# A two-layer decoder trunk on one core: one weight split of layer B's output projection is queued behind the exponentials of the fourteenth head

## The chip, the cores and the metric

The kernel runs on one core of a Trainium2 chip. Its engines have queues of their own and wait for each other through semaphores: TensorE (PE: matmuls and transposes; PEld: its weight loads), VectorE (DVE), ScalarE (ACT), GpSimd (POOL), and SyncE (SP), which issues most of the DMA loads. The metric is the device time of one execution in microseconds; it was 991.41 us before the change, as the median of three runs (990.88 to 992.49).

## The reference, cut to what matters

Two layers over 512 tokens of width 1024, all in float32. Layer A has latent attention and an MLP. Layer B, where the change lies, has sliding-window attention with 16 query heads on 4 key/value heads, each with a learned sink, then the output projection `w_o`, a layer norm and another MLP.

```python
def _swa(x, w_q, sinks, w_o, k_band, v_band, rel_bias):
    q = (x @ w_q).reshape(B, nb, BLOCK, SWA_KV_HEADS, G, SWA_HEAD_DIM)
    s = jnp.einsum('bnqkgd,bnjkd->bnkgqj', q, k_band).astype(jnp.float32) * SWA_HEAD_DIM ** -0.5
    ...
    s = jnp.where(mask[None, :, None, None], s + bias, -jnp.inf)
    m = jnp.maximum(s.max(-1), sink)
    p = jnp.exp(s - m[..., None])
    denom = p.sum(-1) + jnp.exp(sink - m)
    p = (p / denom[..., None]).astype(x.dtype)
    o = jnp.einsum('bnkgqj,bnjkd->bnqkgd', p, v_band).reshape(B, S, SWA_Q_HEADS * SWA_HEAD_DIM)
    return o @ w_o
...
x = _layernorm(alpha * x + y, ln_mix_g[l], ln_mix_b[l])
x = _layernorm(alpha * x + _mlp(x, mlp_w_up[l], mlp_w_down[l]), ln_mlp_g[l], ln_mlp_b[l])
```

## The kernel before

**Products in two parts.** Every float32 operand is split into a high part that the matrix unit takes and a low part, what is left: `split` (line 75) copies on ACT (line 77) and subtracts on DVE or POOL (line 81). A product is then three matmuls, high by high, high by low and low by high (`three`); all matmuls are written by `group` (line 105), so that one line of the profile holds nearly all of PE.

**The weights' stream.** All weights come as chunks of 128 by 1024 in one list, `stream`, in the order of their use. `queue` (line 128) appends a chunk: its `make` loads it into a `raw` tile (two buffers; the load is issued on SP, line 142) and splits it into `wh` and `wl` (four buffers each). Whoever needs a chunk calls `weights`, which takes the next one and first prepares chunks until four are on the way. `queue` has an argument `after`: the name of an instruction kept in `state`, and `behind` then makes every instruction of the split that runs on that instruction's engine stand behind it in that engine's order (an edge of order, no wait for its end). For layer B the list has two chunks of `w_k`, two of `w_v`, eight of `w_sq` (the queries) and eight of `w_so` (the output projection), then the MLP's. The low parts of `w_so` are made on POOL for the chunks 0, 1, 2, 6 and 7 (`POOL_SO`), else on DVE. Chunks 6 and 7 are loaded ahead into a tile of their own (line 151).

**The heads.** `run_steps` walks the 16 heads (counted from 0). In step u it writes `scores` of head u + 2, then what is due of a list `fill` (query projections, parts of the output projection, loads), then `turn` of head u, and after every second head `mix` of a pair of heads two steps back.

- `scores`: eight small matmuls into two PSUM banks; DVE puts the window's two halves together (line 1426), adds the bias and takes the maximum (1430), and makes the negative maximum `nb` (1434). `weigh`: ACT takes four exponentials, one for each block of 128 tokens (1440), then the sink's (1445); DVE adds and inverts the sums (1446, 1447), and POOL scales (1449).
- `turn`: PE transposes (1465), ACT and DVE split into `pt` (77, 81), and POOL makes the product with a triangle, `pm` (1469).
- `mix`: matmuls with the values, first into a bank of the pool of two (`tr`), then into one of the pool of six (`mm`), which scores use too; ACT copies a part, `low` (1497), DVE adds, `o` (1499), and ACT and POOL split `o` into `oh` and `ol`.
- `queries`: a projection for two heads; ACT and DVE make `q` (1398, 1399).
- `proj.part(t, kp)`: six matmuls of the output projection for token block t with chunk kp. In the first part, due in step 11, `weights` is called for chunk 0, and chunk 3, the fourth, is prepared: scores of head 13 have then just been written. Chunk 3 itself is multiplied in `proj.finish`, behind all heads.

**What sets the order.** PE's instructions and SP's loads keep the order in which they are written (`pe`). For ACT, DVE and POOL the order is made as the program is built, by a planner that goes through the program with times of its own and puts an instruction into its engine's queue when its operands are ready by those times; edges like that of `behind` bind it. On the chip each engine follows that order strictly: an instruction that waits holds up what is queued behind it.

Of the kernel before, what the change touches and what calls it, by code (L numbers as in the profile page):

```python
# [33 lines left out]
POOL_O, POOL_SO = (0, 2), (0, 1, 2, 6, 7)  # L34
# [14 lines left out]
def build(tc, nc, io, out):  # L49
    with ExitStack() as top:  # L50
# [11 lines left out]
        def nm(s):  # L62
            n_names[0] += 1
            return f"{s}_{n_names[0]}"
# [10 lines left out]
        def split(dst_h, dst_l, src, engine=None, keep=False):  # L75

            high = nc.scalar.activation(dst_h, src, AF.Copy)  # L77
            if keep:
                pe(high)
            with behind(state.pop("open", None)):  # L80
                low = (engine or nc.vector).tensor_sub(dst_l, src, f32(dst_h))  # L81
            if pinned[0] and engine is None:
                pe(low)
            return high, low

        def pe(ins):
            tc.keep_in_program_order(ins)
# [3 lines left out]
        def behind(pair):  # L91

            both = ExitStack()
            for ins in pair or ():
                both.enter_context(tc.issue_after(ins.ins))
            return both
# [20 lines left out]
        def tiles_of_weights(aside=None):  # L117

            if aside:
                return aside()  # L120
            wh = wp.tile([P, 1024], F32R, tag="wh", bufs=4, name=nm("wh"))
            wl = wp.tile([P, 1024], F32R, tag="wl", bufs=4, name=nm("wl"))
            return wh, wl

        def raw_tile():
            return wp.tile([P, 1024], F32, tag="raw", bufs=2, name=nm("raw"))

        def queue(name, ap, low=nc.vector, after=None):


            index = len(stream)

            def make(pieces=1, between=None):
                cols = ap.shape[-1]
                raw = at_hand.pop(index) if index in at_hand else raw_tile()
                wh, wl = tiles_of_weights()
                for j in range(pieces):
                    c = slice(j * cols // pieces, (j + 1) * cols // pieces)
                    if between:
                        between(j)  # L140
                    if index not in fetched:
                        state["load", name] = nc.sync.dma_start(raw[:, c], ap[:, c])
                        pe(state["load", name])
                    with behind((state[after],) if after else None):
                        state["plain"] = split(wh[:, c], wl[:, c], raw[:, c], low)
                return wh, wl

            def fetch(raw):
                at_hand[index] = raw
                fetched.add(index)  # L150
                pe(nc.sync.dma_start(raw[:, : ap.shape[-1]], ap))

            fetchers[index] = fetch
            stream.append((name, make))
            off_ring.append(False)
# [128 lines left out]
        def mlp_stream(l):  # L284
            holds.append(len(stream) + 2)
            def up(q):

                return lambda r, c, jp: io["up"][
                    l, q * 8 + 4 * c + 2 * jp : q * 8 + 4 * c + 2 * jp + 2, :, r * 512 : (r + 1) * 512
                ].rearrange("c p x -> p c x")  # L290

            def down(q):
                return lambda r, c, jp: io["down"][l, q * 8 + 4 * c + 2 * (1 - r) + jp].rearrange(
                    "p (a b) -> p a b", a=2
                )

            add = {("U", q): queue_seven("up", "U", up(q)) for q in range(NFF)}
            add |= {("D", q): queue_seven("down", "D", down(q)) for q in range(NFF - 1)}
            preloads.append(add["U", 0].preload)
            for i, (which, q, n) in enumerate(steps_of()):  # L300
                if i < 2:
                    add[which, q](n, [lambda j=2 * i + jp: aside_of(j) for jp in range(2)])
                else:
                    add[which, q](n)
            for c in range(8):
                queue("down", io["down"][l, (NFF - 1) * 8 + c])
# [8 lines left out]
            queue("w_sq", io["w_sq"][m], nc.gpsimd if m > 1 else nc.vector)  # L315
        first_so = len(stream)
        for c in range(8):
            queue("w_so", io["w_so"][c], nc.gpsimd if c in POOL_SO else nc.vector)
        mlp_stream(1)

        ready = {}
        state = {"next": 0, "at": 0, "hold": 0}
# [637 lines left out]
        with tc.tile_pool(name="mla", bufs=1) as mp:  # L960
# [212 lines left out]
            for t, rs in ((0, (0, 1)), (1, (0, 1)), (0, (2,)), (1, (2,)), (2, range(3)), (3, range(3))):  # L1173
# [3 lines left out]
                for r in rs:  # L1177
                    wh, wl = ws[r // 2]
                    c = slice((r % 2) * 512, (r % 2 + 1) * 512)
# [136 lines left out]
        with tc.tile_pool(name="swa", bufs=1) as mp:  # L1316
# [87 lines left out]
            def scores(h, _):  # L1404
# [17 lines left out]
                for n2 in range(2):  # L1422
# [4 lines left out]
                    for a in range(2):  # L1427
# [5 lines left out]
                        )  # L1433
                nc.vector.tensor_scalar(nb, mx, sink8[:, h : h + 1], -SWA_SCALE, ALU.max, ALU.mult)
                weigh(h, bs, nb, sm, ri)

            def weigh(h, bs, nb, sm, ri):
                p = mp.tile([P, NT, P], F32, tag="p", bufs=3, name=nm("p"))
                for n in range(NT):
                    nc.scalar.activation(  # L1440
                        p[:, n, :], bs[n // 2][:, n % 2, P:], AF.Exp, bias=nb[:, n : n + 1],
                        scale=SWA_SCALE, accum_out=sm[:, n : n + 1],
                    )
                own = bs[0][:, 0, NT : 2 * NT]
                nc.scalar.activation(own, nb, AF.Exp, bias=sink[:, h : h + 1])
                nc.vector.tensor_add(sm, own, sm)
                nc.vector.reciprocal(ri, sm)
                with tc.high_priority():
                    muls[h] = nc.gpsimd.tensor_mul(p, p, ri.unsqueeze(2).broadcast_to([P, NT, P]))
                ps_of[h] = p  # L1450
# [194 lines left out]
```

## Time and profile before

| | |
|---|---|
| runs, median (lowest to highest) | 991.41 us (990.88 to 992.49) |
| the profiled execution: time / span of the trace | 993.6 us / 991.8 us |
| mean granted PE clock | 0.996 |
| PE busy | 981.9 us (99%) |
| DVE busy | 770.5 us (78%) |
| ACT busy | 544.7 us (55%) |
| POOL busy | 238.9 us (24%) |
| head exponentials (line 1440), first to last start | 539.4 to 616.8 us |

Times in the views are microseconds from the start of the span. In a timeline row stand start, duration, engine, line, operation, then the tiles written and read; brackets give the engine's idle time before it and what ended that. The granted clock is the share of the TensorE clock that the throttle let through.

### The profile page before, as it was taken

How to read it: one execution, taken by the hardware profiler on the slowest of the kernel's cores; microseconds unless marked ns; L12 is line 12 of the kernel's file. 1: busy time of each engine (PE TensorE's matmuls, PEld its weight loads, DVE VectorE, ACT ScalarE, POOL GpSimd, SP SyncE). 2: the span in 40 equal slices, each digit the busy share in tenths (PEclk: the TensorE clock that was granted, in tenths of full speed). 3: DMA queues.
4: the chain of work that ended last, by engine and by line, in shares of the span. 5: the costliest groups of instructions: out<-in, count | busy, mean ns of one | idle time of the engine just before them, and what ended most of it. 6: DMA issues, size and time to landing. Idle time of an engine off the chain costs nothing.

```text
span 991.8 us, 15665 instructions
## 1 busy us (share of the span) xinstructions
PE 981.9 (99%) x6028; PEld 883.7 (89%) x6028; DVE 770.5 (78%) x1279; ACT 544.7 (55%) x842; POOL 238.9 (24%) x207
## 2 busy tenths in 40 slices
PE   9999999999999999999999998999999999999998
PEld 9888888998999999998898987889998998999986
DVE  6589858989768769786686787698885986898756
ACT  5557644467547547646146786436763663664620
POOL 0231101121212212210002996512121122023000
PEclk9999999999999999999999998999999999999999
DMA  7431236399779977964132223328996796898332
GB/s 262 138 95 43 89 124 199 57 221 235 139 192 233 169 166 222 228 108 147 65 107 96 86 83 141 113 58 140 279 182 120 235 213 118 222 261 146 85 128 85
DMA packets 60678, 149.54 MB, mean 151 GB/s; under 512 B 5259, under 2 KB 10300, under 8 KB 60604
## 3 DMA queue, kind: packets, MB, share of 16 engines
q0 software_dynamic: 24320, 58.73, 33.4%
q1 hardware_dynamic: 36140, 89.56, 26.0%
q8 instruction: 47, 0.77, 0.3%
q10 hardware_dynamic: 144, 0.26, 0.1%
q14 instruction: 27, 0.22, 0.1%
HBM read 146.41 MB, written 4.22 MB: 152 GB/s over the span
## 4 chain that ended last, share of the span: by engine, by line
PE 97%; DMA 1%; DVE 1%; POOL 0%; ACT 0%; issue 0%; SPq 0%; DVEq 0%; POOLq 0%
PE mm L105 89%; PE tr L105 5%; PE tr L1243 1%; DMA raw<-in_w_so 1%; PE tr L742 1%; PE tr L1465 1%; PE tr L507 0%; POOL wl L81 0%; PE tr L1007 0%; PE mm L1148 0%; ACT p L1440 0%; DVE pt L81 0%; DVE mm L1430 0%; DVE x L481 0%; ACT wh L77 0%
## 5 line engine op out<-in xcount | busy, mean ns | idle before, releaser
L105 PE MATMUL mm<-wh,fac 128*128 128x512 f32 (+1 forms) x944 | 292.5, 386 | 0.0
L77 ACT ACTIVATE wh<-wq 128x1024 fp32r<-128x1024 f32 x164 | 173.7, 1060 | 184.6 <-PE mm L105 135.7
L81 DVE TENSOR_TENSOR wl<-wq,wh 128x1024 fp32r<-128x1024 f32 x164 | 199.4, 1221 | 68.2 <-ACT wh L77 67.3
L105 PE MATMUL mm<-xth,wh 128*128 128x256 f32 (+1 forms) x928 | 243.4, 290 | 0.0
L105 PE MATMUL mm<-xth,wl 128*128 128x256 f32 (+1 forms) x800 | 233.3, 292 | 0.0
L105 PEld LDWEIGHTS mm<-wh,fac 128*128 128x128 f32 x944 | 176.3, 188 | 35.5 <-DVE fac L81 0.6
L105 PE MATMUL mm<-xtl,wh 128*128 128x256 f32 (+1 forms) x672 | 197.1, 293 | 0.0
L105 PE MATMUL mm<-wl,fac 128*128 128x512 f32 (+1 forms) x472 | 182.3, 386 | 0.0
L105 PEld LDWEIGHTS mm<-xth,wh 128*128 128x128 f32 x928 | 168.6, 192 | 3.1
L105 PEld LDWEIGHTS mm<-xth,wl 128*128 128x128 f32 x800 | 153.2, 192 | 2.7
L105 PEld LDWEIGHTS mm<-xtl,wh 128*128 128x128 f32 x672 | 128.7, 191 | 3.0
L77 ACT ACTIVATE wh<-raw 128x1024 fp32r<-128x1024 f32 (+3 forms) x86 | 84.9, 989 | 82.6 <-PE mm L105 58.3
L204 POOL DMA_DIRECT2D wq<-in_up x64 | 77.6, 1238 | 200.3 <-DVE wl L81 193.0
L105 PEld LDWEIGHTS mm<-wl,fac 128*128 128x128 f32 x472 | 88.8, 188 | 16.6
L81 DVE TENSOR_TENSOR wl<-raw,wh 128x1024 fp32r<-128x1024 f32 (+2 forms) x64 | 74.4, 1172 | 32.6 <-ACT wh L77 32.4
L204 POOL DMA_DIRECT2D wq<-in_down x48 | 42.0, 874 | 189.1 <-DVE wl L81 183.2
L81 POOL TENSOR_TENSOR wl<-raw,wh 128x1024 fp32r<-128x1024 f32 (+2 forms) x22 | 47.0, 2137 | 90.4 <-ACT wh L77 67.6
L105 PE MATMUL mm<-wh,oh 128*128 128x512 f32 x128 | 51.2, 400 | 0.0
L105 PE MATMUL mm<-wh,ol 128*128 128x512 f32 x128 | 50.6, 395 | 0.0
L105 PE MATMUL mm<-wl,oh 128*128 128x512 f32 x128 | 50.5, 394 | 0.1
L443 POOL TENSOR_TENSOR rs<-mv,half 128x1 f32<-128x1 f32 x16 | 8.8, 552 | 168.1 <-DVE mv L488 163.3
L641 DVE TENSOR_TENSOR x<-mm,x 128x512 f32<-128x512 f32 (+1 forms) x49 | 32.9, 675 | 15.4 <-PE mm L105 15.4
(246 smaller groups left out, 1790.9 us busy)
## 6 DMA issues: line engine op xcount, KB each, us to landing
wq<-in_up POOLq DMA_DIRECT2D x64, 512.0 KB, 7.2
wq<-in_down POOLq DMA_DIRECT2D x48, 512.0 KB, 7.0
wq<-in_up SPq DMA_DIRECT2D x32, 512.0 KB, 6.6
raw<-in_down SPq DMA_DIRECT2D x28, 512.0 KB, 5.7
wq<-in_down SPq DMA_DIRECT2D x24, 512.0 KB, 5.3
raw<-in_up SPq DMA_DIRECT2D x16, 512.0 KB, 4.4
raw<-in_w_o SPq DMA_DIRECT2D x8, 512.0 KB, 3.3
raw<-in_w_sq SPq DMA_DIRECT2D x8, 512.0 KB, 3.2
```

The source lines that it names most:

```text
L77: high = nc.scalar.activation(dst_h, src, AF.Copy)
L81: low = (engine or nc.vector).tensor_sub(dst_l, src, f32(dst_h))
L105: pe(nc.tensor.matmul(dst, st, mv, start=first and i == 0, stop=last and i == len(pairs) - 1, **kw))
L204: state["added", key, a, more, jp] = nc.gpsimd.dma_start(half(a, jp), chunk(*more, jp), accum_op=ALU.add)
L443: state["rs"] = nc.gpsimd.tensor_tensor(r, v, half, ALU.pow)
L641: nc.vector.tensor_add(xs[t][:, c], b, xs[t][:, c])
L742: pe(nc.tensor.transpose(pt[:, a, :], xs[t][:, k * P : (k + 1) * P], ident))
L1243: pe(nc.tensor.transpose(pt[:, kb * P : (kb + 1) * P], p[:, kb * P : (kb + 1) * P], ident))
L1465: pe(nc.tensor.transpose(pt[:, n, :], p[:, n, :], ident))
```

## The change

The fourth chunk of layer B's output weight (`c == 3`) gets an edge: the ACT part of its split, the copy into `wh`, comes behind the exponential that was written last when the chunk is prepared, which is that of the fourth token block of head 13, the fourteenth. The subtraction on DVE needs the copy. Nothing is added or taken out, and no operand changes.

```diff
@@ -315,7 +315,7 @@
         first_so = len(stream)
         for c in range(8):
-            queue("w_so", io["w_so"][c], nc.gpsimd if c in POOL_SO else nc.vector)
+            queue("w_so", io["w_so"][c], nc.gpsimd if c in POOL_SO else nc.vector, "exp" if c == 3 else None)
         mlp_stream(1)
@@ -1437,7 +1437,7 @@
                 for n in range(NT):
-                    nc.scalar.activation(
+                    state["exp"] = nc.scalar.activation(
                         p[:, n, :], bs[n // 2][:, n % 2, P:], AF.Exp, bias=nb[:, n : n + 1],
                         scale=SWA_SCALE, accum_out=sm[:, n : n + 1],
                     )
```

## The prediction

> **What bounds the kernel now.** I read the page first, then the waits and the granted clock around layer B's heads, then the timeline of each engine there.
>
> ```profile
> span 991.8 us, 15665 instructions
> PE 97%; DMA 1%; DVE 1%; POOL 0%; ACT 0%; issue 0%; SPq 0%; DVEq 0%; POOLq 0%
> ```
>
> The chain that ended last is matmuls for 97% of the span: PE is the bound, and any other engine costs time only where PE waits for it. Here it does, in layer B's heads (waits between 590 and 630 us: total, times, longest):
>
> ```profile
> PE mm L105 <- ACT p L1440: 3.1, 1, 3.1
> ```
>
> PE waits once for 3.1 us, for exponentials. The ACT timeline (start, duration, and in brackets the idle time before and what ended it) shows why they are late:
>
> ```profile
> 599.10 0.62 ACT L77 ACTIVATE oh<-o 128x512 fp32r<-128x512 f32 x1
> 601.77 1.06 ACT L77 ACTIVATE wh<-raw 128x1024 fp32r<-128x1024 f32 x1 [2.05 <-DMA raw<-in_w_so]
> 602.86 0.59 ACT L1398 ACTIVATE q<-mm 64x512 fp32r<-64x512 f32 x1
> 603.47 0.37 ACT L1440 ACTIVATE p<-mm,nb 128x128 f32<-128x128 f32 x1
> ...
> 604.51 0.37 ACT L1440 ACTIVATE p<-mm,nb 128x128 f32<-128x128 f32 x1
> ...
> 609.74 0.37 ACT L1440 ACTIVATE p<-mm,nb 128x128 f32<-128x128 f32 x1
> ...
> 611.87 0.60 ACT L77 ACTIVATE pt<-tr 128x512 fp32r<-128x512 f32 x1 [0.96 <-PE tr L1465]
> ```
>
> The copy at 601.77 is the split of w_so's fourth chunk. It stands in ACT's order ahead of the last query copy and of head 12's four exponentials (603.47 to 604.51; heads count from 0, four exponentials each), and waits 2.05 us for its load. Head 13's last exponential is at 609.74: the change puts the copy behind it. What PE pays:
>
> ```profile
> 593.27 0.64 PE L105 MATMUL mm<-pt,vv 128*128 128x256 f32 x4
> ...
> 594.22 0.22 PE L105 MATMUL mm<-skh,q 128*128 128x128 f32 x1
> ...
> 595.15 0.40 PE L105 MATMUL mm<-xth,wh 128*128 128x512 f32 x1
> ...
> 599.28 0.39 PE L105 MATMUL mm<-wh,oh 128*128 128x512 f32 x1
> ...
> 600.67 0.60 PE L1465 MATMUL tr<-ident,p 128*128 128x128 f32 x4
> ...
> 605.03 1.22 PE L105 MATMUL mm<-pt,vv 128*128 128x256 f32 x4 [3.06 <-ACT p L1440]
> ...
> 611.17 0.61 PE L1465 MATMUL tr<-ident,p 128*128 128x128 f32 x4
> ...
> 614.13 0.70 PE L105 MATMUL tr<-pt,vv 128*128 128x512 f32 x2 [0.92 <-DVE pt L81]
> ```
>
> Besides the 3.06 us, what follows is slow. PE in equal windows (length, busy, count, granted clock, DMA share, GB/s):
>
> ```profile
> 600.93:604.34 3.41, 1.04 (x8) 1.00 0.77 305
> 604.34:607.76 3.42, 2.73 (x13) 0.50 0.46 165
> 607.76:611.17 3.41, 3.41 (x12) 0.50 0.00 0
> 611.17:614.58 3.41, 2.49 (x19) 1.00 0.00 0
> ```
>
> After a window with 1.04 us of work the granted clock is 0.50 for 6.83 us. From 605.03 to 611.17 PE does the second half of a mix, one head's scores and one projection part. At full clock these take 0.95 (593.27 to 594.22), 0.93 (594.22 to 595.15) and 1.39 us (599.28 to 600.67), 3.27 together; here 6.14. So the clock costs **2.87**, the stall **3.06**, together 5.93 us.
>
> **The change, part by part.** *Removed ahead of head 12:* the query copy can start at 599.72, where oh ends, instead of 602.86. It takes 0.61 to the first exponential, the fourth starts 1.04 later (604.51 less 603.47), and PE went on 0.52 after that start (605.03 less 604.51): 601.89. PE gets there at 601.97 (605.03 less 3.06). The stall goes whole, with it the nearly idle window, and with that the slow clock: PE could be at the transposes of head 12 (before: 611.17) at 605.24.
>
> *What is late next: DVE.* Its order (start, duration):
>
> ```profile
> 602.86 1.22 DVE L81 TENSOR_TENSOR wl<-raw,wh 128x1024 fp32r<-128x1024 f32 x1 [1.80 <-ACT wh L77]
> 604.00 0.29 DVE L1430 CUSTOM_DVE_ANT_0 mm<-mm,bias 128x128 f32<-128x128 f32 x1
> ...
> 606.38 0.84 DVE L1499 TENSOR_TENSOR o<-tr,low 64x256 f32<-64x256 f32 x2
> 607.99 0.30 DVE L1426 COPY_PREDICATED mm<-upper,mm 128x128 f32<-128x128 int16 x1 [0.77 <-PE mm L105]
> ...
> 608.41 0.19 DVE L1434 TENSOR_SCALAR nb<-mm,sink 128x4 f32<-128x4 f32 x1
> 608.85 0.43 DVE L1426 COPY_PREDICATED mm<-upper,mm 128x256 f32<-128x256 int16 x1 [0.24 <-PE mm L105]
> ...
> 611.11 0.17 DVE L1447 RECIPROCAL ri<-sm 128x4 f32<-128x4 f32 x1
> 612.27 0.30 DVE L1426 COPY_PREDICATED mm<-upper,mm 128x128 f32<-128x128 int16 x1 [0.99 <-PE mm L105]
> ...
> 613.29 0.69 DVE L81 TENSOR_TENSOR pt<-tr,pt 128x512 fp32r<-128x512 f32 x1
> ```
>
> DVE is free at 601.06 (602.86 less the 1.80 that it waits) and would go straight to the row of 604.00. Up to pt at 613.29, whose end PE awaits at 614.13, its work is four stretches: 604.00 to 607.22 (3.22), 607.99 to 608.60 (0.61), 608.85 to 611.28 (2.43), 612.27 to 613.98 (1.71); the gaps between are waits for the slow PE. Back to back they are 7.97, so pt ends at 609.03 and PE goes on 0.15 later (614.13 less 613.98), at 609.18. The gain there is 4.95 instead of 5.93: 0.98 goes to DVE's pace. POOL's scalings do not bind later than that:
>
> ```profile
> 608.67 1.04 POOL L1449 TENSOR_TENSOR p<-p,ri 128x512 f32<-128x512 f32 x1 [5.79 <-DVE nb L1434]
> ...
> 611.45 1.04 POOL L1449 TENSOR_TENSOR p<-p,ri 128x512 f32<-128x512 f32 x1
> ```
>
> Scaling of head 12 to end of scaling of head 13 is 3.82 (with a tri product between), and began 0.26 after the row of 608.41, which moves to about 604.70: it ends near 608.8, ahead of 609.18 less the 0.35 of head 13's transposes.
>
> *Added behind head 13:* the copy, 1.06 on ACT, and the subtraction that needs it, 1.22 on DVE, both now inside the stretch that binds. No row shows them there, so bounds. At best the subtraction stands behind pt and the copy ahead of nothing urgent: 0, gain 4.95. At worst the copy also stands ahead of the sink's exponential, which the sums and the reciprocal of head 13 need: head 13's nb ends with the second stretch, at 604.89, its exponentials take 1.41 (603.47 to 604.88), so the copy runs from 606.3 to 607.4, while DVE is near the end of the third stretch, at some 606.8; it waits 0.6 more, and the subtraction's 1.22 comes on top: gain 3.1. I take the subtraction alone, 1.22: it was put directly behind its copy in the order of before (row 602.86), and the copy's end near 607.5 lies before the pt row's turn. Queued behind the copy are the mix's oh and pt (611.87), behind the subtraction the next head's nb and pt, and behind pt PE. **4.95 − 1.22 = 3.7 us.** A gain beyond 4.95 has no place: DVE has no idle left in that stretch.
>
> *The load behind it.* The chunk's raw buffer comes free with the subtraction, and the sixth chunk's load waits for that (rows of SP, ACT, the chain of waits and PE in turn):
>
> ```profile
> 604.11 0.33 SPq L142 DMA_DIRECT2D raw<-in_w_so  x1
> 634.86 0.33 SPq L457 DMA_DIRECT2D gb<-in_ln_mix_g  x1
> 632.93 2.08 ACT L77 ACTIVATE wh<-raw 128x1024 fp32r<-128x1024 f32 x2
> 593.82 7.93 DMA raw<-in_w_so
> 629.64 0.40 PE L105 MATMUL mm<-wh,oh 128*128 128x512 f32 x1
> ```
>
> Its issue moves from 604.11 to about 609. SP's next issue behind it is at 634.86 and its reader among the copies from 632.93, so it costs nothing while it lands within some 20 us; the fourth chunk's load took 7.93 (chain of waits). The chunk itself is first multiplied in the projection's finish, which begins at 629.64 with the last token block's share of the first three chunks.
>
> *Afterwards* PE is dense; from 612 us to the end its only waits of some length for other engines are
>
> ```profile
> PE tr L105 <- DVE pt L81: 0.9, 1, 0.9
> PE mm L477 <- ACT diag L476: 0.9, 1, 0.9
> ```
>
> so a gain at 614.13 reaches the end. By the profiled execution: span 991.8 to 988.1, its time 993.6 to 989.9. The runs' median lies 2.2 under the profiled time; taken off it, 991.41 − 3.7 = **987.7**.
>
> **Rivals.** *1. The clock falls again.* With 3.7 won, PE does 2.04 us of work (614.13 less 611.17 less 0.92) between 605.24 and 610.4 and idles 3.1 in pieces. A window of 3.41 there holds some 1.2 to 1.7 us of work, between the 1.04 that lost the clock and the 2.49 that kept it. If it is lost, 6.83 us at half clock cost about 3: gain 0.7, 990.7. For: the margin above 1.04 is thin. Against: the idle is broken by transposes and scores. [...]
>
> *2. The untimed difference:* the runs are 2.2 faster than the profiled one; if they kept the clock through the stall, before has PE there earlier, with DVE binding at 604.00 + 7.97 + 0.15 = 612.1; after 610.4: gain 1.7, 989.7. Against: the same stall stands in every run.
>
> *3. Slower: the split slips to the projection's finish.* The edge says only "not before". If the order puts the pair beside the next splits (copies from 632.93, less the 4.95 then won: 627.98), the subtraction ends 1.06 + 1.22 later, at 630.3, the sixth chunk's load lands 7.93 after that and is split by 640.5. PE wants it after eight projection parts of 1.39 from 629.64, at 640.8, less 4.95: 635.8. A stall of 4.7 and the half clock behind it, some 3, against 4.95: +2.7, 994.1. It decides once the subtraction ends after about 626. Against: ACT is idle for 0.96 ahead of 611.87, with the chunk long landed.
>
> **How the numbers follow.** Forecast 0.55 (987.7; its own range 986.3 to 988.5, from 4.95 and 3.1 with 0.2 for the median), rival 1 0.20, rival 2 0.10, rival 3 or another late wait 0.10, rest 0.05. Something under 0.2% (2 us) cannot be told from none. Faster: the forecast, part of rivals 1 and 2, and part of the rest, 0.68; same 0.20; slower 0.12. Range 986.2 to 991.6: the upper end holds rivals 1 and 2.
>
> **What would show it.** Right: the copy behind head 13's exponentials with no wait for the load, no stall before the mix near 602, granted clock 1.00 from 600 to 618, PE's new waits under pt and under head 13's transposes, and the matmuls of 614.13 at 609.2 to 611. Wrong: a granted clock of 0.50 anywhere in the heads, a wait for w_so behind 630, or another engine's order changed beyond the moved pair.

## The result, and the profile after

| | before | after |
|---|---|---|
| runs, median (lowest to highest) | 991.44 us (990.67 to 992.56, 20 runs) | 992.84 us (992.28 to 994.17, 20 runs) |
| profiled execution: time / span | 993.6 / 991.8 us | 992.69 / 990.9 us |

The ratio after to before is 1.0015, 95% interval 1.0009 to 1.0022: 1.4 us slower. The interval leaves out 1, so the change is clear of noise, though it lies within the 0.2% that the prediction took as not to be told from none. The prediction was 987.7 us, range 986.2 to 991.6. The profiled execution of after is 0.9 us shorter than that of before while its runs are longer; why that is no contradiction is settled by the fourth experiment.

The page of after, its span and its chain of waits:

```profile
span 990.9 us, 15666 instructions
...
PE 96%; DVE 1%; POOL 1%; ACT 1%; issue 0%; DVEq 0%; POOLq 0%; ACTq 0%
```

PE still is the bound; POOL and ACT, at 0% before, now have 1% each of the chain. (The one instruction more than before is a semaphore instruction on DVE.) The waits between 590 and 630 us (total, times, longest):

```profile
PE mm L105 <- DVE o L1499: 2.9, 1, 2.9
...
PE tr L1465 <- POOL p L1449: 1.5, 1, 1.5
```

The waits of 3.06 us for exponentials and 0.92 for `pt`, 3.98 together, have become two others, 4.40 us together. PE's timeline:

```profile
601.80 0.74 PE L105 MATMUL mm<-pt,vv 128*128 128x256 f32 x4
...
605.18 0.60 PE L1465 MATMUL tr<-ident,p 128*128 128x128 f32 x4
...
605.96 0.28 PE L105 MATMUL mm<-skl,q 128*128 128x256 f32 x1
609.14 0.36 PE L105 MATMUL mm<-skh,q 128*128 128x256 f32 x1 [2.90 <-DVE o L1499]
...
611.34 1.12 PE L1465 MATMUL tr<-ident,p 128*128 128x128 f32 x4 [1.50 <-POOL p L1449]
612.11 1.20 PE L105 MATMUL tr<-pt,vv 128*128 128x512 f32 x2
```

The old stall is gone: the second half of the mix follows at 601.80 with no wait, and head 12's transposes come at 605.18. Then PE stops in the middle of head 15's scores, whose second half needs what `o` releases, and again ahead of head 13's transposes. Why `o` is late stands in ACT's and DVE's timelines. ACT of after:

```profile
603.51 0.37 ACT L1440 ACTIVATE p<-mm,nb 128x128 f32<-128x128 f32 x1 [0.47 <-DVE nb L1434]
...
604.55 0.37 ACT L1440 ACTIVATE p<-mm,nb 128x128 f32<-128x128 f32 x1
...
604.90 1.06 ACT L77 ACTIVATE wh<-raw 128x1024 fp32r<-128x1024 f32 x1
605.99 0.59 ACT L1497 ACTIVATE low<-mm 64x512 f32<-64x512 f32 x1
606.48 0.25 ACT L1445 ACTIVATE mm<-nb,sink 128x4 f32<-128x4 f32 x1
```

and of before, where the mix's `low` had its turn ahead of head 13's exponentials:

```profile
607.34 0.59 ACT L1497 ACTIVATE low<-mm 64x512 f32<-64x512 f32 x1 [1.10 <-DVE o L1499]
608.70 0.37 ACT L1440 ACTIVATE p<-mm,nb 128x128 f32<-128x128 f32 x1 [0.77 <-DVE nb L1434]
```

With the copy out of the way, the planner put head 13's exponentials first, the copy behind them, and `low` third. (That the exponentials came out earlier by the planner's own times is inferred from the order; no trace holds these times.) The matmuls that `low` reads end at about 603 us (the scores behind them start at 602.85), so it starts 3 us after it could, behind exponentials and copy; ACT even idles 0.47 us ahead of those exponentials, waiting for `nb`. DVE of after:

```profile
606.67 1.23 DVE L81 TENSOR_TENSOR wl<-raw,wh 128x1024 fp32r<-128x1024 f32 x1
607.82 0.22 DVE L1434 TENSOR_SCALAR nb<-mm,sink 128x4 f32<-128x4 f32 x1
607.95 0.29 DVE L1430 CUSTOM_DVE_ANT_0 mm<-mm,bias 128x128 f32<-128x128 f32 x1
...
608.16 0.84 DVE L1499 TENSOR_TENSOR o<-mm,low 64x256 f32<-64x256 f32 x2
609.03 0.16 DVE L1446 TENSOR_TENSOR sm<-mm,sm 128x4 f32<-128x4 f32 x1
609.11 0.68 DVE L81 TENSOR_TENSOR pt<-tr,pt 128x512 fp32r<-128x512 f32 x1
...
609.91 0.17 DVE L1447 RECIPROCAL ri<-sm 128x4 f32<-128x4 f32 x1
```

`o` stands behind the moved subtraction, and head 13's sum and reciprocal behind `o`. POOL's scaling of head 13 starts at 610.25 and ends at 611.29, PE's transposes start at 611.34. The chain of waits that ended last runs through these rows, from the exponentials over copy, `low`, subtraction, `o`, sum, `pt` and reciprocal to the scaling. The granted clock, in equal windows (length, PE busy, count, clock, DMA share, GB/s):

```profile
604.33:607.74 3.41, 1.91 (x13) 1.00 0.05 22
607.74:611.15 3.41, 0.71 (x4) 1.00 0.43 154
611.15:614.57 3.42, 3.23 (x13) 0.50 0.00 0
614.57:617.98 3.41, 3.41 (x19) 1.00 0.00 0
```

Of the 4.40 us of waits 2.70 fall into one window, which is left with 0.71 us of work, and the next one is granted half the clock.

### The profile page after: what moved, and what is told of

Its sections match the earlier page's. It is cut to its first block, busy times and chain, and to the rows that moved or that the text cites. A ratio compares the mean times of both kernels' runs of the same rounds, so it can differ in the third digit from the quotient of the medians.

```text
span 990.9 us, 15666 instructions
## 1 busy us (share of the span) xinstructions
PE 980.6 (99%) x6028; PEld 883.1 (89%) x6028; DVE 770.4 (78%) x1279; ACT 544.4 (55%) x842; POOL 238.7 (24%) x207
## 4 chain that ended last, share of the span: by engine, by line
PE 96%; DVE 1%; POOL 1%; ACT 1%; issue 0%; DVEq 0%; POOLq 0%; ACTq 0%
PE mm L105 88%; PE tr L105 5%; PE tr L1243 1%; PE tr L742 1%; POOL wl L81 1%; PE tr L1465 1%; PE tr L507 0%; ACT wh L77 0%; ACT p L1440 0%; PE tr L1007 0%; DVE mm L1430 0%; DVE pt L81 0%; DVE o L1499 0%; PE mm L1148 0%; DVE q L1399 0%
```

## The experiments

Seven runs follow, two of them of the kernels before and after once more, in two batches; each batch ran on one chip, beside the kernel before. The first four ask whether the moved pair itself costs the time, or whether the heads' own work on ACT, DVE and POOL sets the pace once the load's wait is gone, and whether the clock term of the prediction was there to be won. The last three ask whether the pair's time costs, or its place in the order.

**e1: the pair taken out of the heads.** On after: chunks 3 and 4 are loaded when they were, and split only in step 13, so that chunk 3's copy comes behind head 15's exponentials.

```diff
+            def fetch_only(i):
+                state["hold"] = first_so + 3
+                fetchers[i](raw_tile())
+            def split_now():
+                state["hold"] = len(stream)
+                for _ in range(2):
+                    prep(state["next"])
+                    state["next"] += 1
+            fill.append((0, 11, 11, lambda: fetch_only(first_so + 3)))
...
+                if (t, kp) == (0, 1):
+                    fill.append((0, 12, 12, lambda: fetch_only(first_so + 4)))
...
+                    fill.append((0, 13, 13, split_now))
```

> The loads of chunks 3 and 4 stay where they are in SP's order; their splits are written two steps later and chunk 3's copy is queued behind the exponentials of head 15. ACT's order in heads 12 to 14 is that of the changed kernel (sink of head 12 early, head 13's exponentials ahead of the mix's second low) without the copy between them. Theory 1 (the moved pair itself, 1.06 us on ACT and 1.22 on DVE ahead of low and o, makes PE wait): the wait of scores for o falls from 2.90 us to under 0.6, that of head 13's transposes for p from 1.50 to under 1.0, the granted clock stays 1.00 from 600 to 618 us, and the time is 988 to 989.5 us. Theory 2 (the rest of the new order, exponentials ahead of low, costs it): the waits stay above 3 us in sum and the time is 992 to 993.

Measured: 990.32 us (989.19 to 991.37) against 991.45 for before; ratio 0.9989 (0.9980 to 0.9998). PE's waits, and POOL's timeline ahead of the second:

```profile
606.89 0.36 PE L105 MATMUL mm<-skh,q 128*128 128x256 f32 x1 [0.41 <-DVE o L1499]
...
609.80 0.66 PE L1465 MATMUL tr<-ident,p 128*128 128x128 f32 x4 [2.20 <-POOL p L1449]
```

```profile
607.48 1.27 POOL L81 TENSOR_TENSOR ol<-o,oh 128x512 fp32r<-128x512 f32 x1 [1.69 <-ACT oh L77]
608.71 1.04 POOL L1449 TENSOR_TENSOR p<-p,ri 128x512 f32<-128x512 f32 x1
```

Without the pair the wait for `o` falls from 2.90 to 0.41 us, so the pair made it. Head 13's exponentials still stand ahead of `low` here:

```profile
604.78 0.37 ACT L1440 ACTIVATE p<-mm,nb 128x128 f32<-128x128 f32 x1
605.27 0.59 ACT L1497 ACTIVATE low<-mm 64x512 f32<-64x512 f32 x1
```

So it is the copy between the two, and the subtraction ahead of `o`, that cost; the place of the exponentials accounts for at most the 0.41 us that are left. The second wait grows from 1.50 to 2.20 us with no pair near: it belongs to the heads. POOL scales head 13 behind the mix's `ol`. Theory 1 was right on the pair alone; it expected under 1.0 us for this second wait, and 988 to 989.5 us.

**e2: the load early, the pair where it was before.** On before: chunk 3's load is issued ahead of the last query projection.

```diff
+                    if (m, part) == (7, 1):
+                        fill.append((0, -9, -9, lambda: fetchers[first_so + 3](raw_tile())))
```

> The kernel before, with chunk 3's load issued ahead of the last bias load, so that it has landed some 6 us before its copy; no edge. The copy then stands ahead of the query copy of head 14, near 598 us, and does not wait. Theory A (before, only the wait for the load hurts, not the copy's place ahead of head 12): PE's 3.06 us wait falls under 0.7, no window with clock 0.50, time 988 to 989.5. Theory B (the copy's and subtraction's own time ahead of head 12 holds up DVE and PE too): a wait of 1 to 2 us remains, time 990 to 991.4.

Measured: 992.04 us (991.20 to 992.59); ratio 1.0004 (0.9995 to 1.0013). The copy no longer waits for its load (it starts at 597.29), yet PE waits 1.34, 0.39 and 2.20 us, 3.93 together:

```profile
602.02 0.70 PE L105 MATMUL tr<-pt,vv 128*128 128x512 f32 x2 [1.34 <-DVE pt L81]
...
607.53 0.36 PE L105 MATMUL mm<-skh,q 128*128 128x256 f32 x1 [0.39 <-DVE o L1499]
...
610.44 0.66 PE L1465 MATMUL tr<-ident,p 128*128 128x128 f32 x4 [2.20 <-POOL p L1449]
```

So the load's wait, taken alone, was worth nothing: the heads' chain fills the place. Its last two waits are those of e1. Theory B's wait of 1 to 2 us came; its time, 990 to 991.4, did not, since the 2.20 us, and a window at half clock behind them, were not in it.

**e3: the subtraction on POOL.** On after, `POOL_SO` takes chunk 3.

```diff
-POOL_O, POOL_SO = (0, 2), (0, 1, 2, 6, 7)
+POOL_O, POOL_SO = (0, 2), (0, 1, 2, 3, 6, 7)
```

> The changed kernel with chunk 3's subtraction on POOL (2.4 us there, where POOL sits idle for 4.7 us) instead of DVE (1.22); the copy stays behind head 13's exponentials, ahead of low. If copy and subtraction both hold up o: the wait of scores for o is 1.5 to 1.9 us instead of 2.90 and the time 991.0 to 991.8. If the copy ahead of low does it alone: 2.6 us or more stays, time 992.5 to 993.

Measured: 991.66 us (990.63 to 992.16); ratio 0.9999 (0.9990 to 1.0008). The wait for `o` is 1.77 us instead of 2.90, 1.13 less, near the 1.23 of the subtraction and within the 1.5 to 1.9 expected if both hold up `o`; that for head 13's scaling stays at 1.50. Of the 2.49 us that the pair adds to the wait for `o` (2.90 less e1's 0.41), the subtraction thus makes some 1.1 and the copy some 1.4.

**e4: before, once more.**

> The kernel before, unchanged, to see its runs one by one. If the profiled execution of 993.6 us lost the clock for two windows and most executions for one or none: most runs have a mean granted clock of 0.997 or more and a span near 989.6 us, and those of 0.996 or less lie 1.5 to 3 us above. If the clock loss is the same in all: the mean clock is 0.996 in all, whatever the span.

Measured: 991.01 us (990.47 to 992.10); ratio 0.9997 (0.9988 to 1.0006). Its profiled execution took 991.22 us, span 989.4, 2.4 less than that of the front table. PE waits 2.39, 0.24 and 1.20 us; the first, and the clock in equal windows:

```profile
604.34 0.74 PE L105 MATMUL mm<-pt,vv 128*128 128x256 f32 x4 [2.39 <-ACT p L1440]
```

```profile
600.38:603.80 3.42, 1.57 (x10) 1.00 0.85 344
603.80:607.21 3.41, 2.73 (x19) 1.00 0.48 163
```

The same stall, shorter since the load landed sooner (ACT waited 1.37 us for it instead of 2.05), and no slow clock behind it. Of 67 runs of before beside the experiments (e4's own among them), 24 show a mean granted clock of 1.000, at 990.28 to 991.65 us (median 990.74); 33 show 0.998 or 0.997 (median 991.58); only 10 show 0.996 or less, at 992.9 to 994.0 (median 993.48). The profiled 993.6 us, at 0.996, is like that last group, which lies 2.7 us above the first, near the 2.87 of the prediction; the median of all 67 lies 0.7 above it. Of 31 runs of after none shows more than 0.998, which is the mean of its profiled execution with one slow window. A mean of 0.998 can come from elsewhere, though: the clock also falls to 0.50 behind PE's last matmuls, for 1.75 us of the span in the trace of before and 0.88 in that of after. The last matmul ends 3.99 us ahead of the end of the span in both, so by an estimate from these traces half the clock there takes at most 0.002 off the mean. The 0.997 or less of 23 of the 31 runs needs more than that.

**e5: the same pair, one instruction later.** On after: the edge is to the sink's exponential of head 13 instead of its last exponential of scores.

```diff
-                    state["exp"] = nc.scalar.activation(
+                    nc.scalar.activation(
                         p[:, n, :], bs[n // 2][:, n % 2, P:], AF.Exp, bias=nb[:, n : n + 1],
...
-                nc.scalar.activation(own, nb, AF.Exp, bias=sink[:, h : h + 1])
+                state["exp"] = nc.scalar.activation(own, nb, AF.Exp, bias=sink[:, h : h + 1])
```

> The change with one edge moved by one instruction: the copy comes behind head 13's exponential of the sink instead of its last exponential of scores. The order on the engines then is: the mix's second low and the sink's exponential ahead of the copy, o, sum and reciprocal of head 13 ahead of the subtraction, and POOL's scaling of head 13 ahead of ol. The same pair, the same load, the same two heads. Theory A (what costs the time is that low, o and head 13's sum stand behind the pair): o ends near 606.4 instead of 609.0, so PE's 2.90 us ahead of the second half of head 15's scores shrinks to about 0.5, and the 1.50 ahead of head 13's transposes to about 1.2; no clock loss in most runs; span near 987.5, median 989 to 990, ratio 0.997 to 0.999. Theory B (the pair's 2.3 us of ACT and DVE cost the same wherever they stand among heads 12 to 15): waits of 4 us in all, the clock lost as in the change, 992 to 993.

Measured: 990.31 us (989.11 to 991.31) against 991.60 for before; ratio 0.9984 (0.9975 to 0.9993). ACT's order and PE's waits:

```profile
604.70 0.60 ACT L1497 ACTIVATE low<-mm 64x512 f32<-64x512 f32 x1
605.20 0.25 ACT L1445 ACTIVATE mm<-nb,sink 128x4 f32<-128x4 f32 x1
605.38 1.04 ACT L77 ACTIVATE wh<-raw 128x1024 fp32r<-128x1024 f32 x1
```

```profile
606.32 0.36 PE L105 MATMUL mm<-skh,q 128*128 128x256 f32 x1 [0.41 <-DVE o L1499]
...
609.06 0.66 PE L1465 MATMUL tr<-ident,p 128*128 128x128 f32 x4 [2.03 <-POOL p L1449]
609.47 0.71 PE L105 MATMUL tr<-pt,vv 128*128 128x512 f32 x2
```

`low` is ahead of the copy, `o`, sum and reciprocal of head 13 ahead of the subtraction. The wait for `o` is 0.41 us, as in e1 with no pair there at all: theory A. The second wait, expected at 1.2, is 2.03, for a reason of its own (last section). Theory A was wrong on the clock: this execution lost it for a window, and 6 of 11 runs show a mean of 0.997, which the end of the trace alone does not make. So the median, too, lies above the 989 to 990 expected.

**e6: e1 with POOL's and DVE's order set.** The subtraction of head 12's `pt` comes behind head 13's reciprocal, `ol` behind head 13's scaling.

```diff
-                nc.vector.reciprocal(ri, sm)
+                ri_of = nc.vector.reciprocal(ri, sm)
+                if h == 13:
+                    state["ri"] = ri_of
...
+                if h == 12:
+                    state["open"] = (state["ri"],)
                 split(whole[:, 0], whole[:, 1], pt)
...
+                if h == 9:
+                    state["open"] = (muls[13],)
                 split(oh[m // 4][:, m % 4, :], ol[m // 4][:, m % 4, :], o.rearrange("p a b -> p (a b)"), nc.gpsimd)
```

> The late split of e1 with two more edges: the subtraction of head 12's pt behind head 13's reciprocal on DVE, and ol of the mix behind head 13's scaling on POOL. Theory A (e1's remaining wait of 2.20 us ahead of head 13's transposes is DVE's and POOL's order: reciprocal at 607.99 behind pt, scaling at 608.71 behind ol): reciprocal near 607.4, scaling near 607.6 to 608.6, wait about 1.1; span near 986.9, median near 989.2, ratio about 0.9978. Theory B (the heads' sum of ACT, DVE and POOL work sets the pace, whatever the order): the wait comes back under the mix or the next head's pt, and the median stays at 990.3 like e1.

Measured: 988.80 us (988.34 to 989.98, 7 runs) against 991.60; ratio 0.9970 (0.9959 to 0.9981), faster than both kernels. POOL's timeline and PE's (the added lines make line 1449 into 1451 here, and 1465 into 1467):

```profile
607.00 1.04 POOL L1451 TENSOR_TENSOR p<-p,ri 128x512 f32<-128x512 f32 x1 [1.90 <-PE mm L105]
607.99 1.28 POOL L81 TENSOR_TENSOR ol<-o,oh 128x512 fp32r<-128x512 f32 x1
```

```profile
608.09 0.66 PE L1467 MATMUL tr<-ident,p 128*128 128x128 f32 x4 [1.22 <-POOL p L1451]
608.50 0.71 PE L105 MATMUL tr<-pt,vv 128*128 128x512 f32 x2
```

Scaling and `ol` changed places, and the wait went from 2.20 to 1.22 us: theory A. Nothing came back later (between 590 and 630 us PE has only this wait and 0.41 for `o`), so the heads' sum of work was not the limit in e1, the order was.

**e7: after, once more.**

> The changed kernel again, beside the other two on one chip, as the level to compare them with. Both theories: 992.5 to 993, ratio near 1.0015; waits of 2.90 and 1.50 us in the profile and a stretch of half clock behind 611 us.

Measured: 993.14 us (992.60 to 994.26); ratio 1.0014 (1.0005 to 1.0022); PE's waits 2.90 and 1.50 us, the slow clock for two windows; the time is a little above the 992.5 to 993 expected.

**The sum.** The nine profiled executions, in us: the waits of PE over 0.2 between 600 and 615, and half of PE's busy time in the windows there at clock 0.50.

| | span | PE's waits | half of slow work | span less both |
|---|---|---|---|---|
| before | 991.8 | 3.06 + 0.92 | 3.07 | 984.8 |
| e4 (before) | 989.4 | 2.39 + 0.24 + 1.20 | 0 | 985.6 |
| after | 990.9 | 2.90 + 1.50 | 1.62 | 984.9 |
| e7 (after) | 992.0 | 2.90 + 1.50 | 2.77 | 984.8 |
| e1 | 987.9 | 0.41 + 2.20 | 0 | 985.3 |
| e2 | 990.0 | 1.34 + 0.39 + 2.20 | 1.71 | 984.4 |
| e3 | 990.2 | 1.77 + 1.50 | 2.67 | 984.3 |
| e5 | 988.7 | 0.41 + 2.03 | 1.71 | 984.6 |
| e6 | 986.6 | 0.41 + 1.22 | 0 | 985.0 |

Spans that differ by 5.4 us come to one level within 1.3: these waits and the clock are nearly the whole difference. The six rows with a slow clock lie lowest (984.3 to 984.9, the others 985.0 to 985.6), so half of the slow work, which is an estimate, takes the clock's price a little too high.

## Why the prediction was wrong, point by point

- **The stall of 3.06 us goes: right.** The mix follows at 601.80 (forecast 601.97), head 12's transposes at 605.18 (forecast 605.24).
- **The slow clock, 2.87 us: the first failed step.** It was there in the profiled execution, and was booked as a gain for every run: "The runs' median lies 2.2 under the profiled time; taken off it, 991.41 − 3.7". Its size was about right, but only 10 of 67 runs of before pay it in that size (e4); by the medians there the term was worth some 0.7 us to a typical run, not 2.87. The 2.2 us that the text set aside were the sign of it. Rival 2 said so, at 0.10.
- **The pair's cost: the step that turned the sign.** "At worst the copy also stands ahead of the sink's exponential" left out `low`. The bound took ACT's order of before as given, with `low` ahead of head 13's exponentials; the planner makes that order anew, and in after the two are turned around. That alone costs at most 0.41 us (e1); but the copy, tied to the exponentials, came ahead of `low` with them. So `o` came behind copy and subtraction, and PE waited 2.90 us for a row that is no term of the sum. The last paragraph of the prediction names this, "another engine's order changed beyond the moved pair", as what would make it wrong; the sum had no price for it, though the whole cost lay there. e5 prices it: the same pair, one instruction later, and PE's waits are 2.44 instead of 4.40 us. By the ratios to before of e1, which has no pair there, and of after (0.9989 and 1.0015), the pair cost some 2.6 us with the clock that went with it, where the sum booked 1.22 and its bound 1.85.
- **DVE's pace, 0.98 us, and POOL's scalings that "do not bind": about right in size, wrong in what binds.** The traces begin this stretch up to 0.7 us apart, so it is counted here from the mix's second half. With neither stall nor pair the matmuls after head 13's transposes were to come 7.21 us later (601.97 to 609.18), and with the subtraction 8.43. In e6, with POOL's order set and no pair, they come after 7.19 us (601.31 to 608.50); in e1, late through POOL's order, after 8.19; in e5, with the pair there, after 8.01; in after 10.31. But in none of the four does PE wait for `pt`, DVE's row in the sum: its last wait is each time for POOL's scaling, which the sum had put at 608.8, hardly ahead of the 608.83 at which it would bind. That e6 meets the figure is in part luck. What made e1 and after late was that somebody else's instruction was queued first.
- **Rival 1, the clock falls again: right in what happens,** at 0.20; its time, 990.7, was not. Both profiled executions of after lose it in the heads (for one and for two windows), and no mean clock of the 31 runs speaks against the same there, though a mean can't tell where it was lost. The window holds 0.71 us of work rather than the 1.2 to 1.7 worked out, since the waits are longer.
- **Rival 3 and the load behind the pair: no trace of either.** The sixth chunk's load is issued at 607.93 (forecast about 609), and no matmul waits for a weight after 615 us (one weight load waits 0.5 us, as it did before).

The sign of the runs then follows: a typical before pays its 3.8 us of waits and no slow clock (24 of 67 runs) or little of it (33), after pays 4.4 us and, as far as its runs show, the slow clock each time.

## What to carry to other kernels

An edge on one instruction in a planned order is a change of the whole order behind it: list, for each engine, which instructions could now pass which, and price the worst such swap on the path (here `low` behind a copy) before summing durations. A term that only one profiled execution shows (here a granted clock) is a gain only as often as the runs pay it; when the median lies 2 us under the profiled time, look for that term first. When a stall goes, the next chain sets the pace at once: the pair out of the heads gave 1.1 us (e1), and two edges that put the reciprocal and the scaling first more than doubled that to 2.8 (e6).

## What the runs showed of the hardware that was not expected

**How little it takes to lose the clock, and how it differs from run to run.** In the traces of before and after the clock changes only at whole multiples of 3.413 us from each other: between the changes lie 6.83 and 378.88 us in before (2 and 111 times), 3.41 and 375.47 in after (1 and 110 times). In the heads the clock stays at 0.50 for 3.41 us in e2 and e5 and for 6.82 and 6.83 in e3 and e7. The grid does not lie alike in every execution: counted from the start of the span, a window ends at 611.15 in after and at 610.04 in e7, which is the same kernel. The window ahead of a fall held 1.04 (before), 0.71 (after, e7), 1.22 (e2), 1.65 (e3) or 1.38 us of matmuls (e5); windows with 1.57 (e4, above), 1.51 (e1), 1.91 (after, above) and 2.19 (e6) kept the clock. For e4, e1 and e6, where the clock stays at 1.00 in the heads, the place of the windows is an estimate, by the same grid. Behind the last matmuls the clock fell after windows that held 1.12 (before) and 0.31 us (after). So these traces show no sharp bound in this measure: 1.65 us lost the clock, and 1.57 and 1.51 kept it. Once at 0.50, a window with 2.73 us of slowed work (before) did not win the clock back; one with 3.23 (after) did. Where the grid falls on the waits seems to have decided: e5's wait of 2.03 us, all in one window, lost the clock; e1's of 2.20, partly in the window before, did not.

**DVE's large subtraction and POOL's work held each other up.** In e5 head 13's scaling and the moved subtraction overlap. The rows of POOL's line 1449 grouped (shortest/median/longest, ns), and the two in their timelines:

```profile
L1449 POOL TENSOR_TENSOR p<-p,ri x16: 1028/1041/1841, 541.5 to 614.8; 128x512 f32<-128x512 f32 x16
```

```profile
606.91 1.20 DVE L81 TENSOR_TENSOR wl<-raw,wh 128x1024 fp32r<-128x1024 f32 x1
```

```profile
607.16 1.84 POOL L1449 TENSOR_TENSOR p<-p,ri 128x512 f32<-128x512 f32 x1 [1.91 <-ACT pt L77]
```

One of the 16 scalings took 1.84 us instead of 1.04, the one that began 0.25 us after the subtraction; it ends 0.89 us after the subtraction does (609.00 less 608.11). The 0.80 us more is the 0.8 us by which e5's second wait, 2.03, passed the 1.2 expected. The trace of before has it in both directions, behind the heads:

```profile
632.46 1.23 DVE L81 TENSOR_TENSOR wl<-raw,wh 128x1024 fp32r<-128x1024 f32 x1
633.10 1.73 POOL L81 TENSOR_TENSOR ol<-o,oh 128x512 fp32r<-128x512 f32 x1 [3.38 <-ACT oh L77]
634.01 1.91 DVE L81 TENSOR_TENSOR wl<-raw,wh 128x1024 fp32r<-128x1024 f32 x1 [0.33 <-ACT wh L77]
```

`ol`, begun while the first subtraction ran, takes 1.73 us against a median of 1.29, and the second subtraction, begun while `ol` ran, 1.91 against the 1.23 of the first. In e4 the chunk's own subtraction took 1.77 us instead of 1.22, begun while POOL's `pm` ran. In these four cases it is the one that starts second that takes longer, by some 0.15 us less than the time in which both were under way: 0.80 for 0.95 us in e5, 0.44 for 0.59 and 0.68 for 0.82 in before, 0.55 for 0.69 in e4. So a large subtraction on DVE and POOL's work cost each other time here, which neither the prediction nor the expectations had counted.
